# A hybrid encoder block on one core: the program that orders its instructions is given another load rate, several passes and one more place

## The chip, the cores and the metric

One core of one Trainium2 chip runs the whole block in one launch. The metric is the device time of a run in microseconds (us), as a median over several runs. All arithmetic is in 32-bit floats; products on TensorE are made exact enough by splitting each factor into a high and a low part and multiplying three times.

## The reference, cut to what matters

x is 1024 positions by 1024 channels; there are 256 memory positions and one layer.

```python
h = rms_norm(x, pre_mix_g);  z = h @ w_in + b_in              # 1024 -> 1792 columns
y_a = pool_mixer(z[:, :256], pool_w, pool_scale)              # trailing means of 2, 4, 8, 16
y_b = spatial_gating_mixer(z[:, 256:1024], sg_ln_g, sg_ln_b, sg_w, sg_b)
y_c = conformer_conv_mixer(z[:, 1024:], conv_w, conv_b, conv_ln_g, conv_ln_b)  # 31 taps
x = x + rms_norm(concat(y_a, y_b, y_c) @ w_out, post_mix_g)
h = rms_norm(x, pre_x_g);  m = rms_norm(mem, mem_g)
x = x + rms_norm(memory_cross_attention(h, m, wq, wk, wv, wo), post_x_g)       # 4 heads
h = rms_norm(x, pre_ff_g)
x = x + rms_norm(square(relu(h @ w_ff1)) @ w_ff2, post_ff_g)                   # 4096 wide
```

## The kernel before, in words

The kernel is written as a straight list of operations, and that list isn't executed in the order in which it is written. A class `Schedule` records each operation (`record`) with its engine, an estimated cost (`_cost`), the operations it depends on, and the tiles that it touches. When all are recorded, `emit` calls `order`, which goes through a simulated clock and works out one order for all engines; the program is then emitted in that order. So each engine has a fixed queue of instructions, and on the chip it runs them in that order, waiting wherever an operand isn't there yet. Every instruction therefore carries the same line number in the profile, L161 (the call in `record`), and instructions are told apart by the names of their tiles.

The order is found greedily. For each engine, among the operations whose dependencies are all placed, `pick` takes the one with the earliest possible start; among those with the same start the one with the earliest due time. That start takes in the engine's own free time, the operands' ends plus a latency by pair of engines (`LAT`; 2100 ns behind a DMA), a lock between VectorE and GpSimd for operations that use the port they share (`op.port`), and a place for every tile that is not yet live. Due times come from a pass over the operations in the order in which they are written: TensorE's operations are due one after the other by their summed costs, all others as late as what follows them allows, going backwards along the dependencies. TensorE itself takes ties in the order of writing.

A DMA is modelled as the "sync" engine: one transfer at a time, with the cost bytes / 360 (in ns; 360 GB/s, at least 450 ns), so 1456 ns for 512 KB. On the chip, SyncE's queue only issues the transfers, and many are under way at once. A load can also not be issued before the matmul that stands 150 matmuls back in the written order (`LEAD`) has ended.

Most tiles of 4 KB per partition live in a common stock of places (`slots`, `slot`; `NS` = 49). A tile takes a place at its first operation and gives it back after its last one. Statistics of a few columns have places of their own (`small`, 24 of each width), and a few constants stand by themselves, among them `pw`, the weights of the pooling mixer split in two (2 KB per partition).

The stages, with the names that the rows use:

- Input: blocks `x` are loaded, normalised, transposed (`p0t`) and scaled into `h`. Products with `zc0` to `zc2` give the convolution's input (`zg`, `za`).
- Mixers, about 33 to 270 us: `zb` is the product with rows `zr0` to `zr7` of w_in; ScalarE copies its first part into `zt`, which TensorE transposes (`zat`) into `zaT` for the pooling mixer (`zw`, `zp`, `ph`, `pya`); VectorE forms `zz` and `yb`, transposed in `ybt`; VectorE also adds the 31 taps of the convolution in `cacc`. In the same stretch the memory tokens are transposed (`memt`, `mT`) and multiplied with wk and wv (`wkp`, `wvp`).
- The rows of wk, wv and w_out arrive as `wk0r`, `wv0r`, `out0r` and so on: SyncE loads 512 KB, ScalarE makes the high part (`wk0h`), GpSimd the low part (`wk0l`, two instructions).
- Output projection: `omp`, then per block a residual and norm (`omx`, `omt`) and transposes `om0t` to `om7t`.
- Attention: `pq` (query product, done with seven half-size products in place of eight), `sc`, softmax (`mx`, `pt`), transposed weights `pT`, `o`, and the output product `ox` with weights `wob`, `wow`, `wot`.
- Dense layer: first part `fx`, `fy`, `fz` (seven half-size products; left factors `h3a10h` to `h3a71l`, right factors `w1o` from loads `w1a` to `w1d`), whose results (`c`, `sa`, `sb`) are written to DRAM as `scr_hid`; second part `g` with loads `w2a` to `w2d` and `ha` (read back from `scr_hid`), accumulated in `acc`, and the last residual in `fx` (`finish`).

Of the kernel before, what the change touches and what calls it, by code (L numbers as in the profile page):

```python
# [11 lines left out]
F32R = mybir.dt.float32r  # L12
# [4 lines left out]
P = 128  # L17
# [9 lines left out]
WINDOWS = (2, 4, 8, 16)  # L27
TAPS = 31
LEAD = 150
NS = 49  # L30


class _Op:
# [32 lines left out]
class Schedule:  # L66
# [13 lines left out]
           "pool": {"act": 75, "dve": 60, "pe": 309, "pool": 102, "sync": 100},  # L80
           "sync": {"act": 2100, "dve": 2100, "pe": 2100, "pool": 2100, "sync": 2100}}
    SLACK = 50000.0
    BYDUE = ("act", "dve", "pool", "sync")
    TABLE = {AF.Sigmoid: "sigmoid", AF.Gelu_apprx_tanh: "gelu", AF.Exp: "exp"}

# [116 lines left out]
    @staticmethod  # L202
    def _cost(eng, method, args, kw, ins):
        n = 1
        for d in args[0].shape[1:]:
            n *= d
        if method == "dma_start":
            return max(450.0, n * args[0].shape[0] * 4 / 360.0)
        size = lambda a: int(np.prod(a.shape[1:]))
        if eng == "pe":  # L210
            return max(109.0, 13.4 + n * 0.4167)
        wide = [a for a in ins if size(a) > 1]
        ptrs = len(ins) - len(wide) if n > 1 else 0
        if eng == "act":
            c = 51.0 + 0.833 * n + (0.0 if ins[0].space == bass.MemoryType.PSUM else 42.0)
            return c + 93.0 * min(ptrs, 1) + (93.0 if "accum_out" in kw else 0.0)
        if eng == "pool":
            if method == "tensor_tensor":
                return 520.0 if n < 17 else 60 + 2.4 * n
            return 60 + 1.0 * n  # L220
        n = max([n] + [size(a) for a in wide])
        psum = any(a.space == bass.MemoryType.PSUM for a in ins + [args[0]])
        if not psum and len(wide) == 1 and method in ("tensor_scalar", "tensor_scalar_mul",
                                                      "tensor_copy"):
            return 69 + 0.52 * n + 61.0 * ptrs
        return 69 + 1.042 * n + 61.0 * ptrs


    def order(self):
        ops, tiles, tags = self.ops, self.tiles, self.tags  # L230
        for i, op in enumerate(ops):
            op.left, op.ready, op.end = len(op.deps), 0.0, None
            for d in op.deps:
                ops[d].users.append(i)


        due, at = [0.0] * len(ops), 0.0
        for i, op in enumerate(ops):
            if op.eng == "pe":
                at += op.cost  # L240
            due[i] = at + (0.0 if op.eng == "pe" else self.SLACK)
        for i in range(len(ops) - 1, -1, -1):
            op = ops[i]
            for u in op.users:
# [2 lines left out]
        for i, op in enumerate(ops):  # L247
            op.due = due[i] if op.eng in self.BYDUE else op.prio
        ready = {e: [] for e in self.ENG}
# [3 lines left out]
        free = {e: 0.0 for e in self.ENG}  # L253
        port = {"dve": 0.0, "pool": 0.0}
        table = None
        out = []
        best = {e: None for e in self.ENG}
# [46 lines left out]
        n = len(ops)  # L304
        while len(out) < n:
            b, be = None, None
            for e in self.ENG:
                if ready[e]:
                    k = pick(e)
# [4 lines left out]
            t0, _, i = b  # L314
            op = ops[i]
# [3 lines left out]
            for t in op.tiles:  # L319
                r = tiles[t]  # L320
                if not r["live"]:
                    r["live"] = True
                    tag = tags[r["tag"]]
                    at = min(tag["free"])
# [11 lines left out]
            for t in op.tiles:  # L336
                r = tiles[t]
# [32 lines left out]
def block_kernel(ctx: ExitStack, tc: tile.TileContext, x, mem, pre_mix_g, w_in, b_in, pool_w,  # L370
# [4 lines left out]
    sc = Schedule(nc, LEAD)  # L375
    act, dve, pool, pe, sync = sc.act, sc.dve, sc.pool, sc.pe, sc.sync

    cp = ctx.enter_context(tc.tile_pool(name="const", bufs=1))
# [5 lines left out]
    junk = cp.tile([P, D], F32, tag="junk", name="junk")  # L384
    sc.slots(sp, NS, junk)

    def slot(name, shape, dt=F32):
        return sc.slot(name, shape, dt)
# [1 line left out]
    def bank(name):  # L390
        return sc.tile(pp, [P, 512], F32, "b", 8, name)

    def small(name, n, bufs=24):
        return sc.tile(mp, [P, n], F32, f"m{n}", bufs, name)

    x, mem, out = x[0], mem[0], out[0]
# [20 lines left out]
    def rstd_of(name, src, n, extra=None):  # L417

        t = small(name + "e", n)
        if extra is None:  # L420
            dve.tensor_scalar(t, src, EPS, None, ALU.add)
        else:
            dve.scalar_tensor_tensor(t, src, EPS, extra, ALU.add, ALU.add)
        r = small(name + "r", n)
        pool.tensor_tensor(r, t, half[:, :n], ALU.pow)
        return r
# [227 lines left out]
    for g in range(4):  # L654
        o = (g % 2) * 64
        sync.dma_start(pwr[o:o + 64, g // 2, o:o + 64], pool_w[0, g])
    pw = sc.tile(cp, [P, 2, 2, P], F32R, "pw", 1, "pw")
    act.copy(pw[:, 0], pwr)
    lo_of(dve, pw[:, 1], pwr, pw[:, 0])
    inv = sc.tile(cp, [P, 2, 16], F32, "inv", 1, "inv")  # L660
# [47 lines left out]
    for hf in range(2):  # L708
# [4 lines left out]
        for pr in range(2):  # L713
# [4 lines left out]
            for i in range(2):  # L718
# [19 lines left out]
                r = rstd_of(f"vr{hf}{b}", mv[:, 1:2], 1)  # L738
# [37 lines left out]
    for t in range(2):  # L776
# [4 lines left out]
        r = rstd_of(f"memr{t}", ms, 1)  # L781
# [512 lines left out]
    for ch in range(2):  # L1294
# [17 lines left out]
        for i, g, first in ((1, 0, True), (2, 1, True), (6, 0, False), (5, 1, True), (7, 0, False),  # L1312
                            (3, 1, False), (4, 0, False)):
            ops = []
# [20 lines left out]
            n = 1 if ch == 1 and i == 4 else 3  # L1335
# [60 lines left out]
```

## Time and profile before

| what | us |
|---|---|
| median of 3 runs | 1198.07 |
| lowest and highest run | 1197.9, 1200.57 |
| the profiled execution's own time | 1196.5 |
| its span from first to last instruction | 1194.8 |

The mean granted TensorE clock over the span is 0.994. The profile is that of one execution. A busy TensorE is one with a matmul under way; an idle stretch is put down to what ended it. The idle stretches of the other engines matter only where TensorE waits for them in the end.

### The profile page before, as it was taken

What the parts mean: (1) busy time and instruction counts of PE and PEld (TensorE: products, weight loads), DVE (VectorE), ACT (ScalarE), POOL (GpSimd) and SP (SyncE); (2) the same over time, 40 slices, a digit from 0 to 9 for tenths busy, and PEclk for the clock granted to TensorE, in tenths of its full rate; (3) what the DMA queues carried; (4) which work ended last, traced back from release to release, by engine and by line L of the source; (5) the groups of instructions that cost most, each with busy time, mean ns of one, the idle gap of its engine ahead of it and who ended that gap; (6) DMA issues with size and microseconds to landing.
All of it is one profiled execution on the core that took longest, in us unless ns stands there. A gap on an engine that the chain in (4) does not pass through costs nothing.

```text
span 1194.8 us, 14793 instructions
## 1 busy us (share of the span) xinstructions
PE 1158.2 (97%) x5387; PEld 957.9 (80%) x5387; DVE 875.1 (73%) x1234; ACT 556.2 (47%) x973; POOL 271.0 (23%) x260
## 2 busy tenths in 40 slices
PE   7999999999999999999999999999999999999997
PEld 6788877787877898788778878888888888888885
DVE  5899999464459757799996877667589744587736
ACT  6422245734566358749833434333364632435421
POOL 5352458894062403443000000000000000000001
PEclk9999999999999999999999999999999999999999
DMA  8400024652240313126043355444685244443443
GB/s 275 152 1 1 1 91 164 243 207 89 88 159 28 114 53 107 58 101 229 36 159 123 141 192 169 159 149 142 211 301 210 89 141 169 167 168 132 144 156 141
DMA packets 86056, 163.11 MB, mean 137 GB/s; under 512 B 6475, under 2 KB 29919, under 8 KB 85983
## 3 DMA queue, kind: packets, MB, share of 16 engines
q1 hardware_dynamic: 85982, 162.17, 39.1%
q8 instruction: 42, 0.69, 0.2%
q14 instruction: 32, 0.25, 0.1%
HBM read 116.01 MB, written 46.14 MB: 136 GB/s over the span
## 4 chain that ended last, share of the span: by engine, by line
PE 76%; DVE 9%; ACT 6%; DMA 4%; POOL 2%; issue 2%; SPq 1%; DVEq 0%; ACTq 0%; POOLq 0%
PE g L161 25%; PE fx L161 13%; PE fz L161 7%; PE zb L161 5%; PE ox L161 4%; PE omp L161 4%; PE pq L161 4%; PE zg L161 3%; PE za L161 2%; PE fy L161 2%; DVE cacc L161 2%; PE wkp L161 2%; ACT h L161 1%; PE sc L161 1%; ACT junk L161 1%
## 5 line engine op out<-in xcount | busy, mean ns | idle before, releaser
L161 POOL TENSOR_TENSOR fr0r<-fr0e,half 128x1 f32<-128x1 f32 x1 | 0.9, 866 | 590.2 <-DVE fr0e L161 590.2
L161 DVE SCALAR_TENSOR_TENSOR cacc<-hc,taps,cacc 128x512 f32<-128x512 f32 (+14 forms) x180 | 121.0, 738 | 0.2
L161 DVE TENSOR_TENSOR c<-c,fz 128x512 f32<-128x512 f32 x32 | 21.8, 684 | 52.2 <-PE fz L161 34.1
L161 DVE TENSOR_TENSOR acc<-acc,g 128x512 f32<-128x512 f32 x40 | 25.8, 681 | 33.1 <-PE g L161 33.1
L161 ACT COPY c<-fx 128x512 f32<-128x512 f32 x48 | 28.4, 596 | 38.6 <-PE fx L161 29.2
L161 ACT ACTIVATE c<-fx 128x512 f32<-128x512 f32 x16 | 9.6, 598 | 61.0 <-PE fx L161 61.0
L161 ACT CAST w1o<-w1a 128x512 fp32r<-128x512 f32 x32 | 20.3, 638 | 29.4 <-DVE sb L161 7.8
L161 DVE SCALAR_TENSOR_TENSOR c<-c 128x512 f32<-128x512 f32 x48 | 32.5, 684 | 0.3
L161 PE MATMUL sc<-kv,q 128*128 128x256 f32 x192 | 30.3, 291 | 0.0
L161 ACT ACTIVATE junk<-acc 128x512 f32<-128x512 f32 x16 | 10.1, 632 | 40.8 <-DVE acc L161 40.6
L161 PE MATMUL fx<-h3a40h,w1o 128*128 128x512 f32 x64 | 25.4, 397 | 2.2 <-ACT c L161 2.2
L161 PEld LDWEIGHTS sc<-kv,q 128*128 128x128 f32 x192 | 26.0, 190 | 0.9
L161 ACT CAST w1o<-w1c 128x512 fp32r<-128x512 f32 x32 | 19.6, 626 | 14.2 <-PE fz L161 5.3
L161 PE MATMUL o<-pT,kv 128*128 128x512 f32 x96 | 24.9, 394 | 1.4 <-DVE pT L161 1.4
L161 PE MATMUL fx<-h3a60h,w1o 128*128 128x512 f32 x64 | 25.3, 401 | 0.0
L161 PE MATMUL fx<-h3a11h,w1o 128*128 128x512 f32 x64 | 25.2, 393 | 0.0
L161 PE MATMUL fz<-h3a30h,w1o 128*128 128x512 f32 x64 | 25.1, 392 | 0.0
L161 PE MATMUL fy<-h3a21h,w1o 128*128 128x512 f32 x64 | 25.0, 393 | 0.0
L161 PE MATMUL fy<-h3a20h,w1o 128*128 128x512 f32 x64 | 24.9, 390 | 0.0
L161 PE MATMUL fz<-h3a50h,w1o 128*128 128x512 f32 x64 | 24.9, 389 | 0.0
L161 PE MATMUL fx<-h3a41h,w1o 128*128 128x512 f32 x64 | 24.9, 389 | 0.0
L161 PE MATMUL fz<-h3a31h,w1o 128*128 128x512 f32 x64 | 24.9, 389 | 0.0
(1555 smaller groups left out, 3991.5 us busy)
## 6 DMA issues: line engine op xcount, KB each, us to landing
ha<-scr_hid SPq DMA_DIRECT2D x56, 512.0 KB
scr_hid<-c SPq DMA_DIRECT2D x48, 256.0 KB
scr_hid<-sa SPq DMA_DIRECT2D x32, 256.0 KB
scr_hid<-sb SPq DMA_DIRECT2D x32, 256.0 KB
x<-in_x_dram SPq DMA_DIRECT2D x8, 512.0 KB
omx<-in_x_dram SPq DMA_DIRECT2D x8, 512.0 KB
scr_x<-omx SPq DMA_DIRECT2D x8, 512.0 KB
wqb<-in_wq_dram SPq DMA_DIRECT2D x8, 512.0 KB
```

The costliest lines, as they stand in the source:

```text
L161: op.fn = lambda: f(*[put(a) for a in args], **{k: put(v) for k, v in kw.items()})
```

## The change

Five things change, and no operation of the computation is added, removed or altered.

- `_cost` of a DMA becomes bytes / 250 in place of bytes / 360, so 2097 ns for 512 KB; the least cost of 450 ns and the latency of 2100 ns stay. It holds for loads and for stores.
- `order` calls the old procedure (now `_order`) six times. The first pass takes TensorE's operations in the order of writing for the due times, as before. Each later pass takes the order in which the pass before it placed TensorE's operations. The pass with the shortest simulated span is emitted. Ties on TensorE itself are still broken by the order of writing.
- The stock of 4 KB places grows from 49 to 50 (`NS`).
- `small` has 20 places of each width in place of 24.
- `pw` is no longer a constant by itself; it takes one of the 4 KB places, from its first write until the pooling mixer's last product.

```diff
--- before.py
+++ after.py
@@ -27,7 +27,7 @@
 WINDOWS = (2, 4, 8, 16)
 TAPS = 31
 LEAD = 150
-NS = 49
+NS = 50
 
 
 class _Op:
@@ -80,6 +80,7 @@
            "pool": {"act": 75, "dve": 60, "pe": 309, "pool": 102, "sync": 100},
            "sync": {"act": 2100, "dve": 2100, "pe": 2100, "pool": 2100, "sync": 2100}}
     SLACK = 50000.0
+    PASSES = 6
     BYDUE = ("act", "dve", "pool", "sync")
     TABLE = {AF.Sigmoid: "sigmoid", AF.Gelu_apprx_tanh: "gelu", AF.Exp: "exp"}
 
@@ -205,7 +206,7 @@
         for d in args[0].shape[1:]:
             n *= d
         if method == "dma_start":
-            return max(450.0, n * args[0].shape[0] * 4 / 360.0)
+            return max(450.0, n * args[0].shape[0] * 4 / 250.0)
         size = lambda a: int(np.prod(a.shape[1:]))
         if eng == "pe":
             return max(109.0, 13.4 + n * 0.4167)
@@ -227,18 +228,47 @@
 
 
     def order(self):
+
+
+        best, pe = None, [i for i, op in enumerate(self.ops) if op.eng == "pe"]
+        for n in range(self.PASSES):
+            out = self._order(pe)
+            self.spans = getattr(self, "spans", []) + [self.span]
+            if best is None or self.span < best[0]:
+                best = (self.span, out, [op.end for op in self.ops],
+                        {k: r["at"] for k, r in self.tiles.items()})
+            pe = [i for i in out if self.ops[i].eng == "pe"]
+        self.span, out, ends, places = best
+        for op, end in zip(self.ops, ends):
+            op.end = end
+        for k, at in places.items():
+            self.tiles[k]["at"] = at
+        return out
+
+    def _order(self, pe_order):
         ops, tiles, tags = self.ops, self.tiles, self.tags
+        for op in ops:
+            op.users = []
         for i, op in enumerate(ops):
             op.left, op.ready, op.end = len(op.deps), 0.0, None
             for d in op.deps:
                 ops[d].users.append(i)
-
-
-        due, at = [0.0] * len(ops), 0.0
+        for tag in tags.values():
+            tag["free"] = [(0.0, i) for i in range(tag["bufs"])]
+        for r in tiles.values():
+            r.update(left=len(r["ops"]), end=0.0, live=False, at=0)
+
+
+        due, at = [None] * len(ops), 0.0
+        for i in pe_order:
+            at += ops[i].cost
+            due[i] = at
+        at = 0.0
         for i, op in enumerate(ops):
             if op.eng == "pe":
-                at += op.cost
-            due[i] = at + (0.0 if op.eng == "pe" else self.SLACK)
+                at = max(at, due[i])
+            else:
+                due[i] = at + self.SLACK
         for i in range(len(ops) - 1, -1, -1):
             op = ops[i]
             for u in op.users:
@@ -390,7 +420,7 @@
     def bank(name):
         return sc.tile(pp, [P, 512], F32, "b", 8, name)
 
-    def small(name, n, bufs=24):
+    def small(name, n, bufs=20):
         return sc.tile(mp, [P, n], F32, f"m{n}", bufs, name)
 
     x, mem, out = x[0], mem[0], out[0]
@@ -654,7 +684,7 @@
     for g in range(4):
         o = (g % 2) * 64
         sync.dma_start(pwr[o:o + 64, g // 2, o:o + 64], pool_w[0, g])
-    pw = sc.tile(cp, [P, 2, 2, P], F32R, "pw", 1, "pw")
+    pw = slot("pw", [2, 2, P], F32R)
     act.copy(pw[:, 0], pwr)
     lo_of(dve, pw[:, 1], pwr, pw[:, 0])
     inv = sc.tile(cp, [P, 2, 16], F32, "inv", 1, "inv")
```

## Rows read from the trace of the kernel before

**Rows 1.** The profile page: span, and busy us (share) xinstructions by engine.

```profile
span 1194.8 us, 14793 instructions
PE 1158.2 (97%) x5387; PEld 957.9 (80%) x5387; DVE 875.1 (73%) x1234; ACT 556.2 (47%) x973; POOL 271.0 (23%) x260
```

**Rows 2.** Waits of TensorE: waiter <- releaser: total us, times, longest us.

```profile
PE gmixp L161 <- DMA gmixr<-in_pre_mix_g_dram: 5.9, 1, 5.9
PE fx L161 <- DVE h3a70l L161: 3.2, 1, 3.2
PE ybt L161 <- DVE zz L161: 2.9, 2, 2.4
PE fx L161 <- ACT c L161: 2.4, 3, 1.5
PE zat L161 <- ACT zt L161: 2.1, 1, 2.1
PE om6t L161 <- DVE omt L161: 1.5, 1, 1.5
PE o L161 <- DVE pT L161: 1.4, 1, 1.4
...
PE pT L161 <- DVE pt L161: 1.3, 1, 1.3
...
PE memt L161 <- ACT zaT L161: 0.7, 1, 0.7
...
PE omp L161 <- POOL out6l L161: 0.3, 1, 0.3
```

**Rows 3.** Windows: length; busy us (count) by engine; clock; DMA share; GB/s.

```profile
182.00:184.00 2.00, 2.00 (x11) 1.65 (x10) 2.00 (x4) 1.06 (x1) 2.00 (x3) 1.00 0.99 338
...
190.00:192.00 2.00, 1.30 (x7) 0.96 (x6) 1.97 (x7) 2.00 (x7) 1.60 (x3) 0.59 0.01 2
...
214.00:216.00 2.00, 2.00 (x7) 1.64 (x7) 0.61 (x2) 1.96 (x3) 2.00 (x3) 0.56 1.04 424
```

**Rows 4.** Timeline of ScalarE: start, us, operation [idle before <- what ended it].

```profile
4.35 1.06 ACT L161 ACTIVATE junk<-x 128x1024 f32<-128x1024 f32 x1 [2.27 <-DMA x<-in_x_dram]
...
186.93 1.04 ACT L161 CAST wk6h<-wk6r 128x1024 fp32r<-128x1024 f32 x1 [0.24 <-DMA wk6r<-in_wk_dram]
187.88 0.37 ACT L161 COPY zt<-zb 128x256 f32<-128x256 f32 x1
...
210.54 1.04 ACT L161 CAST wv3h<-wv3r 128x1024 fp32r<-128x1024 f32 x1 [2.45 <-DMA wv3r<-in_wv_dram]
```

**Rows 5.** Timeline of SyncE's queue: when each transfer was issued.

```profile
0.80 0.86 SPq L161 DMA_DIRECT2D x<-in_x_dram  x2
...
173.66 0.33 SPq L161 DMA_DIRECT2D wk0r<-in_wk_dram  x1
...
179.83 0.33 SPq L161 DMA_DIRECT2D wk6r<-in_wk_dram  x1
...
203.49 0.33 SPq L161 DMA_DIRECT2D wv2r<-in_wv_dram  x1
204.84 0.33 SPq L161 DMA_DIRECT2D wv3r<-in_wv_dram  x1
```

**Rows 6.** Windows, sum from 175 to 271 us.

```profile
sum 96.00, PE 90.05 PEld 72.93 DVE 63.47 ACT 54.03 POOL 83.10; mean PE 12.86 PEld 10.42 DVE 9.07 ACT 7.72 POOL 11.87
```

**Rows 7.** The tile pt (min/median/max ns), then the timeline around 475 us.

```profile
L161 DVE TENSOR_SCALAR pt<-pt,rs x32: 334/349/2540, 434.1 to 481.9; 128x256 f32<-128x256 f32 x32
...
476.06 2.38 POOL L161 TENSOR_TENSOR wot<-wob,wob 128x1024 f32<-128x1024 f32 x1
```

**Rows 8.** Windows at the change from attention to the dense layer.

```profile
550.00:560.00 10.00, 10.00 (x50) 8.28 (x49) 8.98 (x13) 9.97 (x28) 0.55 (x1) 1.00 1.04 336
...
590.00:600.00 10.00, 5.93 (x24) 4.02 (x23) 10.00 (x11) 5.07 (x8) 0.00 (x0) 1.00 0.00 1
600.00:604.00 4.00, 4.00 (x12) 3.13 (x11) 4.00 (x6) 1.33 (x3) 0.00 (x0) 0.58 0.00 0
```

## The prediction

> **What bounds the kernel now.** I read the page's busy times first: TensorE is busy for 1158.2 of 1194.8 us, VectorE for 73% [rows 1]. So the kernel is bound by TensorE, and an order of instructions can win at most the 36.6 us in which TensorE stands idle, and what the idle stretches cost it in clock. No product is added or removed, so nothing else is to be had on that engine.
>
> Second, TensorE's waits [rows 2]. 5.9 us go to the first load at the very start; that is before any order can help. Of those that could move, the largest are `fx <- h3a70l` 3.2, `ybt <- zz` 2.9, `fx <- c` 2.4, `zat <- zt` 2.1, `om6t <- omt` 1.5, `o <- pT` 1.4, `pT <- pt` 1.3 and `memt <- zaT` 0.7: 15.5 us together. In none of them is a DMA named. The releaser is always another engine that came late, and the question is what that one had waited for.
>
> Third, the windows just behind the largest of these idle stretches, for the granted clock. After the `zat` and `memt` waits it is 0.59 over 190 to 192 us, after the `ybt` waits 0.56 over 214 to 216 us [rows 3], after `h3a70l` 0.58 over 600 to 604 us [rows 8]: TensorE at its lower level, 1.2 GHz. Over those last 4 us the share lost is 0.42, so 1.7 us of work. I take 1.7 us for each of the three, an estimate from the one stretch that is seen whole. With it the three idle stretches are worth 2.1 + 0.7 + 1.7 = 4.5 us, 2.9 + 1.7 = 4.6 us, and 3.2 + 1.7 = 4.9 us.
>
> Fourth, the timelines of ScalarE and SyncE's queue, for what made the releasers late. TensorE waited for `zat` until ScalarE had copied `zt` (187.88). Ahead of `zt` in ScalarE's queue stood `wk6h`, which waited for the load of `wk6r`, issued at 179.83, until 186.93 [rows 4, 5]: 7.1 us after the issue. It stood there because the program that made the order believed that this load would be there sooner. At 210.54 ScalarE waits in the same way for `wv3r`, for 2.45 us [rows 4].
>
> **The change part by part.**
>
> *Loads at 250.* A load of 512 KB is now booked at 2.10 us in place of 1.46, with 2.1 us of latency behind it in both. Six of them stand in a row from `wk0r` at 173.66 [rows 5] to `wk6r` (`wk1r` had gone before). By the old booking the last lands at 173.66 + 6 x 1.46 + 2.1 = 184.5; by the new one at 188.3; on the chip it was 186.9. For `wv3r`, the second from 203.49 [rows 5], the old booking gives 208.5, the new one 209.8, the chip 210.5. So where loads come in crowds the old figure was early by about 2 us and the new one is off by 1.4 us late and 0.7 us early. In the first case the sign turns, and that matters: the greedy order gives ScalarE the instruction that can start first, and with the load at 188.3 that is `zt`. The head of the queue no longer blocks. Worth: 4.5 us in full, nothing at the least.
>
> For the stall at 210 the new figure is still a little early, and VectorE's `zz` is late for another reason too (it stands behind `zp`, which runs while GpSimd holds the shared port). Worth: 4.6 us at most, half of it by the chip's own load times.
>
> What is late next if both go? GpSimd. From 175 to 271 us it is busy for 83.1 of 96 us [rows 6], with the low parts of all rows of wk, wv and w_out, and at 270 us TensorE already waits 0.3 us for `out6l` [rows 2]. All of TensorE's work behind the mixers feeds on these low parts, and their number is fixed. So TensorE can come out of this stretch earlier only by as much as GpSimd's 12.9 us of idle time shrink, and part of that is before the first row has landed. I take half of it, 6.5 us, as the cap, and 4.0 us of the 9.1 as the value, since the second stall goes only in part. Ends: 0 and 9.1.
>
> *The same figure elsewhere.* `fx <- c` (2.4 us in three waits) stands behind ScalarE's high parts of loads in the dense layer, and `om6t <- omt` (1.5) behind GpSimd's low part of a load of wq. Sum 3.9 us; they are single waits of the same kind, but the late load isn't always the one ahead, so I take half, 2.0. Ends 0 and 3.9.
>
> *Ties by TensorE's own order.* The due time decides only among instructions of an engine that could start at the same moment, so it counts where an engine is full and has a choice. That is VectorE around 590: busy for 10.00 of 10 us while TensorE does 5.93 [rows 8]. There the choice can bring `h3a70l` ahead of low parts that are needed later, but VectorE's sum of work doesn't shrink. I take 1.0 us of the 4.9, ends 0 and 4.9. Should the first pass turn out the shortest, the passes do nothing, and this 1.0 is lost.
>
> *One more place, `pw` in a place, 20 small ones.* Up to the pooling mixer's end the fiftieth place is taken by `pw`, so there the stock is what it was; only behind 216 us is there one more. In the dense layer's second part TensorE doesn't stall as it is, so it has nothing to win there. The small tiles live for a few instructions of one norm each. I take nothing for all three, covered by SyncE's queue being ahead of its users; if that cover is gone, a load that waits for a place is late by one low part, 1.3 us, either way.
>
> *What the new order breaks.* This isn't an edit at one place: every queue is dealt anew. Waits that come of a slip between plan and chip will come again elsewhere. The tile `pt` shows how: normalising takes 0.35 us, but 2.54 once, while GpSimd's `wot` holds the port [rows 7], and TensorE waits 1.3 us. The three of this family, `om6t`, `o` and `pT`, make 4.2 us now. The new order removes old ones and brings new ones: ends +4.2 (as many again on top) and -2.7 (the last two gone, nothing new). I take a loss of 1.7, nearer to the middle.
>
> *The sum.* 4.0 + 2.0 + 1.0 - 1.7 = 5.3 us. The profiled execution's own time was 1196.5, so 1191.2 by it. That execution is 1.57 us below the median of 1198.07; set against the median the forecast is 1192.8.
>
> **The rivals.**
>
> *A. GpSimd takes it back (same).* The 4.0 us are won at 190 and 212 and lost again by 271, since GpSimd works on without a break. For it: 83.1 of 96 us busy and the 0.3 us wait at its end [rows 2, 6]. Against it: GpSimd itself waits for high parts that stand behind late loads. Time: 1198.07 - (5.3 - 4.0) = 1196.8.
>
> *B. 250 is the wrong figure (same).* The first two loads of x are issued at 0.80, and ScalarE has the first at 4.35 [rows 4, 5], 3.55 us later. The old booking gives 1.46 + 2.1 = 3.56, the new one 4.20. In dense stretches the queues move 338 GB/s at a share of 0.99 [rows 3] and 336 at 1.04 [rows 8]. So for a load by itself and for the sum of many 360 was right; only a single load within a crowd is late. A plan that is too slow puts consumers later in the queues than they need to be, and at the start all waits for loads. It costs about 0.64 us for each load that gates something; with the six further blocks of x, 3.8 us, which come off the gain: 1198.07 - 5.3 + 3.8 = 1196.6. The Trainium skill, in "DMA: Bandwidth & Descriptors", section Specifications, gives about 358 GB/s as the limit of HBM for one core and 368 as a cost model's figure; by that rule 360 should have stayed, and the rates just named agree with it, while the 7.1 us of `wk6r` don't.
>
> *C. The change into the dense layer gets worse (slower).* Between 550 and 560 us the DMA engines are full (share 1.04) and VectorE is at 8.98 of 10; from 580 it has no slack at all [rows 8]. The eight loads of w1 and, ahead of them in the same queue, the four stores of the first half's blocks to `scr_x` are each booked 0.64 us longer; in the plan the last load ends 7.7 us later, and VectorE's low parts and sums of w1 can be put behind the `h3` work. Each us of VectorE's work that moves out of 550 to 570 into 580 to 600 is a us more of TensorE's wait, and a new idle stretch of some us brings the low clock again. Price: 7.7 + 1.7 = 9.4 us, in place of the gain of 1.0 there: 1198.07 - 4.3 + 9.4 = 1203.2. It decides against the change from 4.3 us on, that is, once some 2.6 us of VectorE's work have moved; 550 to 560 has 1.02 us without work for it now. Against it: on the chip the loads land no later than before, and a queue in order loses nothing where its next instruction is ready.
>
> *D. All goes well.* Terms near their good ends under GpSimd's cap: 6.5 + 3.9 + 2.5 = 12.9 us, 1185.2.
>
> **How the numbers follow.** About 0.3% (3.6 us) is what a measurement can tell from no change here, so faster ends at 1194.5 and slower begins at 1201.7. The forecast, 1192.8 with its own range from 1189 to 1196, has 0.47; A 0.18; B 0.10; C 0.18; D 0.07. Faster: 0.40 of the forecast, D, and 0.04 of the others make 0.51. Slower: most of C (0.13) and the part of the forecast's, A's and B's cases in which the collisions are at their bad end, 0.06, make 0.19. The rest, 0.30, is within. The range takes in D's end and C's figure: 1185 to 1204. I choose the forecast for the row of `wk6h`: the largest late releaser is explained by the booked load to within 2 us.
>
> **What would show it.** Right: `zt` ahead of `wk6h` in ScalarE's queue, no `zat` wait, no low clock at 190; TensorE's idle sum near 31 us; `omp` at 270 earlier by about 4 us. GpSimd without idle time between 190 and 270 and `omp` where it was is A. ScalarE's or VectorE's waits at the start longer is B. More than 7 us of TensorE idle between 550 and 610 is C. Wrong altogether would be new waits on DMAs in the dense layer's second part, where TensorE has none now, or another order of products on TensorE that changes what is short in each stretch.

## The result and the profile after

The changed kernel takes 1183.93 us (median; 1182.68 to 1184.12) beside 1197.99 us for the kernel before in the same batch: a ratio of 0.9882, 95% interval 0.9856 to 0.9908. It is 14.1 us faster. The forecast was 5.3 us, and 1183.93 lies below the lower end of the range, 1185.

The page of after, span and busy us by engine:

```profile
span 1182.3 us, 14750 instructions
...
PE 1154.1 (98%) x5387; PEld 957.0 (81%) x5387; DVE 882.1 (75%) x1234; ACT 554.7 (47%) x973; POOL 262.2 (22%) x260
```

Set against [rows 1], the span is 12.5 us shorter. TensorE's idle time accounts for 8.4 of these (36.6 to 28.2 us) and its busy time for 4.1 (1158.2 to 1154.1). The products are the same 5387, so most of the second part is clock. Apart from one over the last 4 to 5 us, which both have, before had three stretches at the lower level and after has one; at 1.7 us each, the prediction's estimate, the two that are gone make 3.4 of the 4.1 us.

TensorE's waits of after (waiter <- releaser: total us, times, longest us):

```profile
PE pT L162 <- DVE pt L162: 4.4, 3, 2.1
...
PE om6t L162 <- DVE omt L162: 1.2, 1, 1.2
...
PE fx L162 <- DVE h3a70l L162: 0.4, 1, 0.4
...
PE omp L162 <- POOL out6l L162: 0.3, 1, 0.3
```

Of the waits in [rows 2], `zat`, `ybt` and `fx <- c` are gone and `h3a70l` has shrunk from 3.2 to 0.4. One has grown: `pT <- pt`, from 1.3 to 4.4.

Windows of after (length; busy us and count of TensorE, its loads, VectorE, ScalarE, GpSimd; clock; DMA share; GB/s), at the places of [rows 3, 6, 8] and in attention:

```profile
175.00:265.00 90.00, 88.11 (x432) 71.00 (x431) 61.47 (x118) 53.39 (x80) 84.13 (x72) 1.00 0.62 216
190.00:192.00 2.00, 2.00 (x9) 1.68 (x10) 1.99 (x4) 2.00 (x4) 2.00 (x4) 1.00 0.00 0
466.00:470.00 4.00, 2.01 (x13) 1.45 (x11) 4.00 (x3) 1.92 (x5) 3.92 (x3) 1.00 0.00 0
470.00:474.00 4.00, 2.64 (x9) 2.20 (x10) 3.96 (x9) 2.12 (x6) 1.06 (x1) 0.61 0.00 0
590.00:600.00 10.00, 9.60 (x41) 7.29 (x40) 10.00 (x12) 4.62 (x8) 0.00 (x0) 1.00 0.33 102
600.00:604.00 4.00, 4.00 (x19) 3.31 (x18) 4.00 (x6) 1.60 (x4) 0.00 (x0) 1.00 0.04 13
```

TensorE no longer falls to its lower clock at 190 and 600 us. It falls at 470 instead, behind a stretch in which GpSimd and VectorE are full and TensorE does 2.01 of 4 us.

**Where the time went.** Every version deals the queues anew, so waits can't be matched one to one. I put the traces on a common scale: each matmul counts as its columns / 2.4 ns plus 11 ns (at least 60 ns), and I read when each kernel has done the same amount of that work. The table gives the change of a kernel's lag against before within each stretch, in us, with the stretches by before's time. Negative is a gain. It is worked out from the matmul starts of one profile per kernel; the last column is the lag at 913 us, after which the spans differ by no more than a few tenths from it. Executions of one kernel differ too, and the profiled one can lie off the median (that of passes_place took 1197.84 us, its median is 1195.72), so a cell of less than some 2 us shows little by itself.

| kernel | to 183 (start) | 183-279 (mixers) | 279-407 | 407-515 (attention) | 515-626 (into the dense layer) | 626-913 | sum |
|---|---|---|---|---|---|---|---|
| after | -0.2 | -6.4 | -1.2 | +4.1 | -5.8 | -3.4 | -12.8 |
| rate_only | 0.0 | -4.8 | +0.4 | +6.1 | +1.0 | -3.0 | -0.4 |
| passes_only | -0.3 | -4.6 | +1.1 | -1.3 | -5.4 | +1.4 | -9.1 |
| place_only | 0.0 | -1.4 | +0.2 | -1.4 | -1.1 | -2.2 | -5.8 |
| rate_place | 0.0 | -4.9 | -0.2 | +2.6 | +3.7 | -3.3 | -2.2 |
| rate_passes | -0.2 | -6.4 | -0.2 | +7.5 | -5.4 | -3.0 | -7.6 |
| passes_place | +0.2 | -0.7 | +2.5 | +2.3 | +0.2 | -2.7 | +1.8 |
| rows_at_250 | -0.1 | -2.2 | +0.7 | 0.0 | +1.0 | +0.3 | -0.3 |
| wo_at_250 | +0.4 | +1.6 | 0.0 | +2.4 | +3.9 | +0.4 | +8.8 |
| zt_first | -0.3 | -0.6 | -0.5 | 0.0 | -0.1 | +2.6 | +1.0 |
| casts_behind | -0.1 | -0.3 | -0.5 | 0.0 | 0.0 | +0.5 | -0.3 |
| wo_at_360 | -0.2 | -6.4 | -1.2 | +5.3 | +1.3 | -3.4 | -4.6 |
| quiet_wo | -0.4 | -6.4 | -0.8 | -2.8 | -5.8 | -3.4 | -19.5 |
| wo4_on_vector | -0.2 | -6.4 | -0.8 | -1.3 | -5.8 | -3.4 | -17.7 |
| pt_on_scalar | -0.3 | -6.4 | -1.3 | +6.6 | -5.8 | -3.3 | -10.5 |
| after_pass3 | -0.3 | -3.5 | +1.8 | +4.3 | -4.2 | -3.2 | -5.0 |
| rate_225 | +8.1 | -3.2 | -1.1 | -0.2 | -6.3 | -2.9 | -5.6 |
| rate_275 | -0.5 | -0.3 | +0.8 | +5.8 | -5.1 | -2.5 | -1.8 |
| rate_300 | +6.3 | -4.5 | +1.1 | -1.0 | -4.0 | -2.0 | -4.0 |

### The profile page after: what moved, and what is told of

The parts are those of the page before. It is cut to its first block, busy times and chain, and to the rows that moved or that the text cites. A ratio compares the mean times of both kernels' runs of the same rounds, so it can differ in the third digit from the quotient of the medians.

```text
span 1182.3 us, 14750 instructions
## 1 busy us (share of the span) xinstructions
PE 1154.1 (98%) x5387; PEld 957.0 (81%) x5387; DVE 882.1 (75%) x1234; ACT 554.7 (47%) x973; POOL 262.2 (22%) x260
## 4 chain that ended last, share of the span: by engine, by line
PE 85%; DVE 8%; ACT 3%; issue 1%; POOL 1%; DMA 0%; DVEq 0%; ACTq 0%; POOLq 0%
PE g L162 26%; PE fx L162 13%; PE fz L162 7%; PE omp L162 6%; PE pq L162 6%; PE zb L162 5%; PE ox L162 4%; PE zg L162 3%; PE za L162 3%; PE fy L162 3%; PE wkp L162 2%; DVE cacc L162 2%; PE wvp L162 2%; PE o L162 1%; PE sc L162 1%; ACT h L162 1%
## 5 line engine op out<-in xcount | busy, mean ns | idle before, releaser
L162 DVE SCALAR_TENSOR_TENSOR cacc<-hc,taps,cacc 128x512 f32<-128x512 f32 (+19 forms) x180 | 122.0, 764 | 0.1
L162 PE MATMUL fx<-h3a10h,w1o 128*128 128x512 f32 x64 | 24.9, 390 | 0.0
L162 PE MATMUL fz<-h3a51h,w1o 128*128 128x512 f32 x64 | 24.8, 389 | 0.0
```

Of the source, the lines that this page charges most:

```text
L162: op.fn = lambda: f(*[put(a) for a in args], **{k: put(v) for k, v in kw.items()})
```

## The experiments

Ratios are to the kernel before within the same batch, with 95% intervals.

### The parts of the change, alone and in pairs

**The rate alone**, on the kernel before:

```diff
-            return max(450.0, n * args[0].shape[0] * 4 / 360.0)
+            return max(450.0, n * args[0].shape[0] * 4 / 250.0)
```

> The kernel before with transfers booked at 250 in place of 360 GB/s, and nothing else. Theory 1 (late loads): the booking removes the waits in the mixers (zat, ybt and the low clock behind them) and in the dense layer, so most of the 14 us is here: 1188 to 1190, without the zat wait, but with the 3.2 us wait for h3a70l at the entry to the dense layer. Theory 2 (passes): the load rate matters little, the time stays within 3 us of 1198. Theory 3 (a new deal): any change of the booking gives another order whose time lies anywhere within 6 us of 1196, with waits that have no pattern.

1195.86 us, 0.9987 (0.9977 to 0.9996).

**The six passes alone**: after with `/ 360.0`, `NS = 49`, 24 small tiles, `pw` in its own place.

> The kernel before with six passes, at 360 GB/s, 49 places, pw by itself. Theory 1 (late loads): the zat and ybt waits behind late loads stay, since the booking is the old one, and only the tie-breaking at the entry to the dense layer gains: 1192 to 1194, the 3.2 us wait for h3a70l gone. Theory 2 (passes): 1186 or less. Theory 3 (a new deal): within 6 us of 1196.

1188.77 us, 0.9930 (0.9916 to 0.9945).

**The place alone**: before with `NS = 50`, 20 small tiles and `pw` in a place.

> The kernel before with 50 places, 20 small tiles and pw in a place; 360 GB/s, one pass. Theories 1 and 2: no stall goes for it, 1196 to 1199. Theory 3 (a new deal): the order changes all the same, so within 6 us of 1196, and the stalls sit elsewhere.

1190.34 us, 0.9942 (0.9925 to 0.9958).

**Rate and place**, which is after with one pass:

```diff
-    PASSES = 6
+    PASSES = 1
```

> The changed kernel with one pass in place of six (250 GB/s, 50 places, pw in a place, 20 small tiles). Theory 1 (late loads): nearly all of the gain stays, 1186 to 1189. Theory 2 (passes): the gain goes, 1194 to 1198. Theory 3 (a new deal): within 6 us of 1192.

1193.79 us, 0.9971 (0.9961 to 0.9981).

**Rate and passes**: after with `NS = 49`, 24 small tiles, `pw` in its own place.

> 250 GB/s and six passes, but 49 places, pw by itself and 24 small tiles. If the three parts add up: 1196.5 - 1.5 - 8.6 = 1187 to 1188. If the loss in attention goes with 250 and the gain at the entry to the dense layer with the passes: mixers 5 to 7 us shorter, attention 4 to 6 longer, the entry 6 shorter, 1187 to 1191. Theory 3 (a new deal): anywhere from 1183 to 1195.

1189.12 us, 0.9934 (0.9917 to 0.9950).

**Passes and place**: after with 360 in place of 250.

> The changed kernel with 360 in place of 250. If the parts add up: 1197.4 - 8.6 - 7.0 = 1181 to 1183, so faster than the changed kernel. If place and passes win the same waits (the entry to the dense layer): 1187 to 1189. Theory 1 in its second form: the zat wait is back (1.7 to 2.1 us), no low clock in attention.

1195.72 us, 0.9989 (0.9979 to 0.9998).

The waits that tell these kernels apart, one fence for each (TensorE's waits of rate_only, then passes_only, place_only, rate_place and passes_place):

```profile
PE pT L161 <- DVE pt L161: 6.0, 4, 2.0
...
PE fx L161 <- DVE h3a70l L161: 3.2, 1, 3.2
```

```profile
PE zat L162 <- ACT zt L162: 1.8, 1, 1.8
```

```profile
PE ybt L161 <- DVE zz L161: 3.2, 2, 2.7
PE zat L161 <- ACT zt L161: 1.7, 1, 1.7
```

```profile
PE fx L162 <- DVE w1o L162: 4.3, 1, 4.3
PE pT L162 <- DVE pt L162: 3.6, 3, 1.9
```

```profile
PE pT L162 <- DVE rs L162: 3.7, 1, 3.7
...
PE fx L162 <- DVE h3a70l L162: 1.8, 1, 1.8
PE zat L162 <- ACT zt L162: 1.7, 1, 1.7
```

Two things follow. First, the parts don't add up. By the medians of each batch, rate alone gives 1.5 us, passes 8.6, place 7.0, which would be 17; the three pairs give 3.6, 8.1 and 1.5; all three give 14.1. Place on top of the rate and passes is worth some 6 us, place on top of the passes is a loss of about 7. No part has a value of its own: each deals the whole order anew.

Second, by stretch there is a pattern nevertheless. The wait of `zat` for `zt` stays at 1.7 to 1.8 us where the rows of wk are booked at 360 (passes, place, and both) and isn't among the long ones where they are booked at 250. The rate alone gives 4.8 us in the mixers, close to the 4.0 forecast for it, and then loses 6.1 us in attention to the wait for `pt`.

### Is 250 a better figure, or another draw?

**225, 275 and 300 GB/s**, with the passes and the place as in after; only the divisor changes.

> The changed kernel with 225 in place of 250 GB/s. If the time follows the booked rate up to the point where it meets the chip's own crowds of loads (6.9 to 7.1 us for one of 512 KB): 1182 to 1186, no zat wait. If each rate is another deal: anywhere from 1180 to 1197.

> The changed kernel with 275 in place of 250 GB/s. If the time follows the booked rate: 1186 to 1188, no zat wait. If each rate is another deal: anywhere from 1180 to 1197.

> The changed kernel with 300 in place of 250 GB/s. If the time follows the booked rate (360: 1195.7, 250: 1183.9): about 1190, with a short zat wait. If each rate is another deal: anywhere from 1180 to 1197.

| rate | 225 | 250 (after) | 275 | 300 | 360 (passes_place) |
|---|---|---|---|---|---|
| us | 1190.93 | 1183.93 | 1194.51 | 1194.17 | 1195.72 |
| ratio | 0.9939 | 0.9882 | 0.9982 | 0.9975 | 0.9989 |
| 95% | 0.9921-0.9957 | 0.9856-0.9908 | 0.9970-0.9993 | 0.9962-0.9988 | 0.9979-0.9998 |

250 stands alone. A figure 10% to either side costs 7 and 10.6 us, while the other four lie within 5 us of each other. If 250 fitted the chip's own rate, I would expect the gain to fall off gently to either side, and in the same stretches. It doesn't: 225 and 300 lose 8.1 and 6.3 us by 183 us, where 250 and 275 lose nothing, and 275 then gains only 0.3 us in the mixers. The loss of the two is an earlier `ybt`, near 157 us, that waits twice for `zz`: 3.0 and 1.9 us at 225, 3.0 and 1.6 us at 300, each with 6.8 us at the lower clock, from 158.1 and 155.1 us. At 275, TensorE waits 3.9 us in the mixers for `mT` and is at the lower clock for 10.2 us from 188.6.

**After with three passes**, `PASSES = 3`.

> The changed kernel with three passes, so that the third pass is emitted in place of the fifth; its simulated span is 2.7 us longer by the procedure's own account. If the choice of the shortest pass carries over to the chip: 1186 to 1188. If a pass is only another deal: anywhere from 1180 to 1196, with the zat wait gone in any case.

1190.15 us, 0.9942 (0.9925 to 0.9959). The order that after uses comes from its fifth pass. The best of three is another, which the ordering procedure itself reckons 2.7 us longer (1170.0 against 1167.2, as each kernel's `order` gives it); on the chip it is 6.2 us longer. The procedure's own spans rank the kernels only loosely. The three orders that it reckons shortest (passes_only 1166.9, after 1167.2, rate_passes 1167.7) are the three fastest of the fourteen that it made, but the next, passes_place at 1168.1, is among the slow ones; and it gives 1175.1 for 225 and 1173.3 for 275, of which the chip runs the first 3.6 us faster.

### Which loads carry the effect

**Only the loads of wk, wv and w_out at 250**, on before, in the recording of an operation:

```diff
         op.cost = self._cost(...)
+        if method == "dma_start" and isinstance(args[0], _Slot):
+            if args[0].name.startswith(("s:wk", "s:wv", "s:out")):
+                op.cost = max(450.0, int(np.prod(form(args[0]).shape)) * 4 / 250.0)
```

> The kernel before with only the loads of the rows of wk, wv and w_out booked at 250; all other transfers stay at 360. Theory 1 in its second form (the booking gains about 5 us in the mixers and loses about 5 in attention): the zat wait is gone, the mixers are 4 to 5 us shorter, attention as before: 1191 to 1194. Theory 3 (a new deal): the gain in the mixers comes, but the stages behind it change too by up to 5 us either way.

1196.83 us, 0.9997 (0.9987 to 1.0006). TensorE's waits:

```profile
PE ybt L161 <- DVE zz L161: 4.1, 2, 3.6
```

`zat` isn't among its waits, as the booked load predicts, and `ybt` takes it over: 4.1 us in place of 2.9. Of the gain of 2.2 us in the mixers, some 0.5 are left at 626 us.

**Only attention's loads of wo at 250**, on before: the same edit with `("s:wob",)`.

> The kernel before with only the eight loads of wo booked at 250. Theory 1 in its second form: everything up to the scores as before, then the waits of the transposes pT for pt grow from 1.3 to 4 to 6 us and a stretch at the low clock comes with them: 1201 to 1204. Theory 3 (a new deal): attention changes by less than 2 us, since the loss of the kernels at 250 came of what the order was before that stage.

1203.84 us, 1.0055 (1.0040 to 1.0070), the only kernel that is clearly slower. TensorE's waits:

```profile
PE fx L161 <- DVE w1o L161: 5.5, 1, 5.5
PE pT L161 <- DVE pt L161: 3.7, 3, 1.9
```

**Only attention's loads of wo back at 360**, on after: the same edit with `("s:wob",)` and 360.

> The changed kernel with the eight loads of wo booked at 360 again. If the 250 for wo alone makes the loss in attention: the pT waits are under 1.5 us, no low clock at 470, 1179 to 1181, faster than both kernels. If any change deals anew and the stage before that stays: mixers as in the changed kernel, then 1180 to 1192.

1190.79 us, 0.9943 (0.9923 to 0.9963). Up to 407 us it runs as after does. Attention doesn't improve (+5.3 against +4.1), and the gain at the dense layer's entry is gone (+1.3 against -5.8). So this one booking can bring the wait for `pt`, but taking it back doesn't take the wait away.

### What the two stalls of the mixers are worth by themselves

**`wk6h` behind `zt`**: before's own order, with ScalarE's `wk6h` moved to right behind the copy of `zt`.

```diff
-        order = self.order()
+        order = list(self.order())
+        # src: ScalarE's wk6h; dst: the next ScalarE instruction on zt11
+        order[src:dst + 1] = order[src + 1:dst + 1] + [order[src]]
```

> The kernel before, its order as it was on every engine, but for one instruction: ScalarE's wk6h goes right behind zt instead of ahead of it. If the late load at the head of ScalarE's queue makes the zat wait: the 2.1 us wait and the low clock at 190 go, TensorE is 4 to 4.5 us earlier there, and 1 to 4 us of it are left at the end (1193 to 1196), since GpSimd or the wait at 212 takes back some. If that wait has another cause (zb itself, VectorE): no change at 190, 1196 to 1199.

1197.10 us, 1.0004 (0.9991 to 1.0018). `zt` now starts at 186.62 in place of 187.88 and the wait of `zat` is 1.1 us in place of 2.1, but the low clock stays, now from 191.2 us: neither of the two cases. 1.6 us of gain reach 626 us. Behind it 2.6 are lost, with a new stretch at the lower clock at 706.6 us.

**`wk5h` and `wk6h` behind `zt`** and the seven ScalarE instructions after it, by the same kind of move.

> The kernel before, its order kept on every engine but ScalarE: the two casts wk5h and wk6h go behind the copy zt and the seven instructions that follow it. If the late load ahead of zt is the whole of the mixers' stall at 190: the zat wait and the low clock at 190 go and TensorE is 4 to 4.5 us earlier by 200, of which 1 to 4 are left at the end, 1193 to 1196. If the stall is shared by more engines, as the move of one cast suggests (it gave 0.9 us by 200): 1 to 2 us, 1195 to 1197, with waits for mT (VectorE) in its place.

1198.03 us, 1.0005 (0.9991 to 1.0019): no change, and above both of the ranges that were given. ScalarE's timeline (start, us, operation [idle before <- what ended it]), with `zt` where after has it:

```profile
185.37 0.37 ACT L161 COPY zt<-zb 128x256 f32<-128x256 f32 x1 [0.23 <-PE zb L161]
...
188.92 1.07 ACT L161 CAST wk5h<-wk5r 128x1024 fp32r<-128x1024 f32 x1
189.86 1.09 ACT L161 CAST wk6h<-wk6r 128x1024 fp32r<-128x1024 f32 x1
```

The `zat` wait and the low clock at 190 are gone, and at 192 us TensorE is 2.2 us ahead. Then come TensorE's and GpSimd's timelines:

```profile
211.74 0.41 PE L161 MATMUL ybt<-ident,zz 128*128 128x128 f32 x2 [2.74 <-DVE zz L161]
```

```profile
197.64 4.11 POOL L161 TENSOR_TENSOR zz<-zz,sgn 128x384 f32<-128x384 f32 x4 [3.99 <-DVE zz L161]
...
208.31 1.71 POOL L161 TENSOR_TENSOR wk5l<-wk5r,wk5h 128x512 fp32r<-128x512 f32 x1
211.35 1.27 POOL L161 TENSOR_TENSOR ph<-zp,ph 128x512 fp32r<-128x512 f32 x1 [1.33 <-ACT ph L161]
212.58 1.29 POOL L161 TENSOR_TENSOR wk5l<-wk5r,wk5h 128x512 fp32r<-128x512 f32 x1
```

`ybt` starts at 211.74; in before it started at 212.00, after 2.39 us of wait. Its operand `zz` comes no sooner for TensorE's being ahead (GpSimd's part of it starts at 197.64, in before at 197.87), and TensorE has nothing to fill in, because GpSimd makes `wk5l` only after `zz` and a `ph`. So a stall taken away at 190 comes back at 210. After's GpSimd does it the other way round:

```profile
190.70 2.56 POOL L162 TENSOR_TENSOR wk5l<-wk5r,wk5h 128x512 fp32r<-128x512 f32 x2
...
194.23 2.55 POOL L162 TENSOR_TENSOR wk6l<-wk6r,wk6h 128x512 fp32r<-128x512 f32 x2
196.72 2.57 POOL L162 TENSOR_TENSOR wk7l<-wk7r,wk7h 128x512 fp32r<-128x512 f32 x2
...
202.89 4.11 POOL L162 TENSOR_TENSOR zz<-zz,sgn 128x384 f32<-128x384 f32 x4 [0.57 <-DVE zz L162]
```

With the low parts of rows 5 to 7 made by 199.3 us, TensorE runs `wkp` without a break up to its `ybt` at 212.30. `zz` is no earlier than in before, but TensorE has worked in the meantime: at 237 us it is 8.0 us ahead.

### What attention loses

After's VectorE and GpSimd around 466 us, then the tile `pt` (min/median/max ns, first and last start):

```profile
465.34 6.13 DVE L162 TENSOR_SCALAR pt<-pt,rs 128x256 f32<-128x256 f32 x4
```

```profile
463.87 2.40 POOL L162 TENSOR_TENSOR wow20l<-wob,wow20h 128x1024 fp32r<-128x1024 f32 x1 [6.41 <-ACT wow20h L162]
466.23 2.41 POOL L162 TENSOR_TENSOR wob<-wob,wob 128x1024 f32<-128x1024 f32 x1
468.72 2.34 POOL L162 TENSOR_TENSOR wot<-wob,wob 128x1024 f32<-128x1024 f32 x1
```

```profile
L162 DVE TENSOR_SCALAR pt<-pt,rs x32: 339/349/2494, 426.2 to 473.7; 128x256 f32<-128x256 f32 x32
```

Four normalisations that need 0.35 us each take 6.13 us, while three of GpSimd's instructions follow one another without a gap. Before has the same three instructions of GpSimd in a row, from 471.21 us, and two of its normalisations fall beside them, of 1.43 and 2.54 us (the second is that of [rows 7]). After has three there, of 1.08, 2.46 and 2.49 us, and one of 2.40 us at 455.2.

**GpSimd kept off**: after, with its eleven two-operand instructions on wo as memsets in the same places of the order, which leaves out part of the output product. A memset takes 0.96 us.

```diff
+        if eng == "pool" and isinstance(args[0], _Slot) and args[0].name[:5] in ("s:wow", "s:wob", "s:wot"):
+            op.fn = lambda: self.nc.gpsimd.memset(put(args[0].bitcast(F32)), 0.0)
```

> The changed kernel with its order unchanged on every engine; GpSimd's eleven two-operand instructions on wo (low parts, differences) are replaced by a memset of the same tile, so the output product is left out in part (its low parts and some factors are zero). If the shared port makes the pT waits (4.4 us, low clock at 470): they go, and the kernel ends 4 to 6 us earlier, 1178 to 1180. If they come of VectorE's own queue or of ScalarE: less than 1.5 us.

1177.40 us, 0.9837 (0.9821 to 0.9853). Windows at the two places:

```profile
466.00:470.00 4.00, 4.00 (x24) 3.46 (x24) 2.99 (x7) 3.42 (x9) 0.00 (x0) 1.00 0.00 0
470.00:474.00 4.00, 4.00 (x21) 3.26 (x21) 2.61 (x4) 4.00 (x7) 1.86 (x2) 1.00 0.01 2
```

TensorE is full in both, at full clock. Attention goes from +4.1 to -2.8 us: the two-operand instructions on GpSimd cost after 6.9 us there.

**Four of them on VectorE**, all work kept:

```diff
+        if eng == "pool" and any(n in args[0].name for n in ("wow10l", "wow20l", "wob000", "wot20")
+                                 if isinstance(args[0], _Slot)):
+            f = getattr(self.nc.vector, method)
```

> The changed kernel, its order kept; four of GpSimd's two-operand instructions on wo, the four that fall into attention (wow10l, wow20l and the differences that form wob and wot), are issued on VectorE instead, at the same place in the order. If the shared port makes the pT waits: VectorE gets 4 x 1.2 us of work but no longer waits some 6 us for the port, the pT waits fall under 2 us, 1179 to 1182, faster than both kernels. If VectorE's own work is what pt waits for: 1184 to 1188.

1179.00 us, 0.9848 (0.9830 to 0.9866), the fastest kernel here with all of the work in it. The page, then the tile `pt`:

```profile
span 1177.4 us, 14744 instructions
...
PE 1152.5 (98%) x5387; PEld 956.7 (81%) x5387; DVE 879.6 (75%) x1238; ACT 554.5 (47%) x973; POOL 253.0 (21%) x256
```

```profile
L165 DVE TENSOR_SCALAR pt<-pt,rs x32: 334/348/355, 426.7 to 470.2; 128x256 f32<-128x256 f32 x32
```

No `pt` takes more than 355 ns, and VectorE's busy time falls, from 882.1 to 879.6 us, though it has four instructions more. By stretch it equals after everywhere but in attention (-1.3 against +4.1). The intervals of the two ratios, each to before in its own batch, overlap by a tenth of a per cent; the two profiled spans differ by 4.9 us.

**The normalisation on ScalarE**, after's order otherwise:

```diff
+        if method == "tensor_scalar_mul" and isinstance(args[0], _Slot) and args[0].name[:4] == "s:pt":
+            op.fn = lambda: self.nc.scalar.activation(put(args[0]), put(args[1]), AF.Copy, scale=put(args[2]))
```

> The changed kernel, its order kept; the 32 normalisations of pt are issued on ScalarE (activation with a scale) in place of VectorE. If the shared port makes the pT waits: ScalarE doesn't use it, the waits for pt fall, but ScalarE gets 32 x 0.37 to 0.48 us more, 12 to 15 us where it has 15 to 20 us idle: 1179 to 1184. If ScalarE becomes the bound there: 1185 to 1190.

1186.41 us, 0.9911 (0.9893 to 0.9929). TensorE's waits:

```profile
PE pT L162 <- ACT pt L164: 3.2, 9, 0.8
```

The long waits and the low clock are gone, but there are nine short ones, and attention loses 6.6 us: ScalarE, which also has the exponentials, has become the one that TensorE follows. 2.5 us slower than after.

## Why the prediction was off

**What bounds it, and the sum.** That the change can win only TensorE's idle time and its clock held: 8.4 and 4.1 us make up the span's 12.5. The idle sum was forecast near 31 us and is 28.2. By stretch, forecast against measured: mixers 4.0 against 6.4; the same figure elsewhere 2.0 against 4.6 (1.2 from 279 to 407 us, 3.4 from 626 on); entry to the dense layer 1.0 against 5.8; collisions -1.7 against -4.1. Every gain was put too low, and the loss too. The sum failed by its largest miss, the third term.

**The entry to the dense layer: the step that failed.** I argued that the choice among ties can bring `h3a70l` forward but that VectorE's work there doesn't shrink, and took 1.0 of 4.9. VectorE is indeed as full as before, 10.00 of 10 us, and yet TensorE does 9.60 of them in place of the 5.93 of [rows 8]. The step from a full VectorE to a wait that mostly stays was wrong: it didn't ask what else TensorE could do until `h3a70l` is there. VectorE's timelines, in before, then after, then passes_only:

```profile
584.17 0.68 DVE L161 TENSOR_TENSOR w1o<-w1t,w1o 128x512 fp32r<-128x512 f32 x1
...
597.94 1.21 DVE L161 TENSOR_TENSOR h3a70l<-h,h3a70h 128x1024 fp32r<-128x1024 f32 x1
599.07 0.68 DVE L161 TENSOR_TENSOR w1o<-w1t,w1o 128x512 fp32r<-128x512 f32 x1
```

```profile
579.61 1.29 DVE L162 TENSOR_TENSOR w1o<-w1t,w1o 128x512 fp32r<-128x512 f32 x2
...
589.42 1.23 DVE L162 TENSOR_TENSOR h3a70l<-h,h3a70h 128x1024 fp32r<-128x1024 f32 x1
...
591.16 1.22 DVE L162 TENSOR_TENSOR h3a50l<-h3s,h3a50h 128x1024 fp32r<-128x1024 f32 x1
```

```profile
585.63 0.68 DVE L162 TENSOR_TENSOR w1o<-w1t,w1o 128x512 fp32r<-128x512 f32 x1
...
590.85 1.22 DVE L162 TENSOR_TENSOR h3a70l<-h,h3a70h 128x1024 fp32r<-128x1024 f32 x1
```

The second `w1o<-w1t` is the low part that the second of two products with `h3a6` (12 matmuls each) needs. In before it comes behind `h3a70l`: TensorE has run 14 matmuls with `h3a6` when it stops for `h3a70l`, and the other ten follow later. In after, passes_only and rate_passes it comes first, and TensorE has run all 24. In after `h3a70l` itself also stands ahead of `h3a50l` and `h3a51l`, which it stood behind, and is 8.5 us earlier, of which 3.7 are the lead that after has at 515 us anyway. But in passes_only and rate_passes it still stands behind both, so that move isn't what the gain needs. An engine that is full still chooses what its consumer gets first.

The runs tie this to the passes. In the first pass the procedure holds the second `w1o<-w1t` due at 566.1 us, behind `h3a70l` at 556.7; in the pass that after uses, at 555.0, ahead of 558.0. On before's scale it starts at 584.2 to 591.3 us in all nine orders with several passes and at 596.8 to 599.0 in the five with one. Seven of the nine gain 4.0 to 6.3 us at the entry, and none of the five more than 1.1. It isn't a law: passes_place, which still waits 1.8 us for `h3a70l`, has +0.2, and wo_at_360, which gains 3.9 us from 590 to 605, has lost it again by 626. Moving the one instruction by itself wasn't tried, so that it is the decisive one is argued and not shown. I also put the place at nothing. By itself it gave 7.0 us, of which 1.1 here, and on top of rate and passes some 6; it deals the order anew like the other parts.

**The mixers: the marks right, the prices wrong.** The marks given for it came true: `zt` at 185.32 stands ahead of `wk6h` at 190.18 in ScalarE's queue, there is no `zat` wait and no low clock at 190:

```profile
185.32 0.37 ACT L162 COPY zt<-zb 128x256 f32<-128x256 f32 x1 [0.42 <-PE zb L162]
...
190.18 1.08 ACT L162 CAST wk6h<-wk6r 128x1024 fp32r<-128x1024 f32 x1
```

But I priced the stalls at 190 and 210 as 4.5 and 4.6 us side by side. casts_behind takes the first away whole and ends where it began: the 2.2 us won at 192 are gone by 212. The other way round, passes_only keeps the first (a `zat` wait of 1.8 us and the lower clock from 188.8), has no `ybt` wait among its long ones, and gains 4.6 us in the mixers, nearly all of it between 205 and 217 us. So taking away the late load that the prediction explained was worth nothing by itself there, and the second stall, of which it hoped for half, was worth its price. In after and in passes_only GpSimd makes `wk5l` ahead of `zz`, and TensorE has work in the meantime; the prediction looked at GpSimd's order only as a cap. That order wasn't moved by itself, and rate_only loses both waits with `wk5l` behind `zz`, so it isn't the only way. As a cap it held well: I allowed 6.5 us, half of GpSimd's 12.9 idle us; its idle time fell to 5.9 (90.00 less 84.13), and of 8.0 us won by 237 us 6.6 remain at 279. So GpSimd takes back 1.4, and at the end TensorE waits 0.3 us for `out6l` as before.

**The same figure elsewhere.** 4.6 us lie 0.7 beyond my end of 3.9. The waits for `c` went, as forecast, but `om6t` is still 1.2. Eleven of the fourteen orders dealt anew gain 2.0 to 3.4 us behind 626, whatever their rate (place_only 2.2, passes_place 2.7, by the table; 225 to 300 from 2.0 to 2.9), so this loss belongs to before's order more than to the figure.

**The collisions.** 4.1 against the bad end of 4.2. The place was the one named, the tile `pt` beside GpSimd, and quiet_wo and wo4_on_vector show the cause: 6.9 us with GpSimd off it, 5.4 of them with four instructions moved. I took 1.7 because I balanced new waits against old ones. Yet attention loses 2.4 to 7.5 us in all six kernels that book wo at 250 (after_pass3 4.3 among them), while passes and place by themselves gain 1.3 and 1.4 there; wo_at_250 shows that this booking alone is enough. It isn't needed, though: passes_place loses 2.3 and wo_at_360 5.3. And a slower booking isn't worse: 225 has -0.2 there, 275 +5.8.

**The rivals.** A was right in kind and small, 1.4 us. B's evidence stands (a load by itself takes what 360 says), its price doesn't: the start is 0.2 us earlier, and in no run with all loads at 250 was it later. The Trainium skill's figure in "DMA: Bandwidth & Descriptors", section Specifications, some 358 GB/s, agrees with the 338 GB/s in the first line of [rows 3]; the 424 of the third line lie above it. C didn't happen in after. rate_place pays 3.7 us at the entry, for `w1o`, as C has it; but wo_at_250 pays 3.9 there for `w1o` too, with its loads of w1 booked at 360, so the longer booking of these loads isn't needed for it. D's 1185.2 is nearest to the result, by other terms: it had 2.5 for the entry and no loss in attention. What I gave too little weight is the spread. The fourteen orders dealt anew here run from 1183.9 to 1203.8 us, and twelve of them are faster than before by their intervals (rows_at_250 can't be told from it, wo_at_250 is slower). So its order was a poor draw among these, and a new one is a draw from about that range.

**Open.** Whether 250 holds anything beyond a lucky draw of the whole order; 225 and 275 speak against it, but three neighbours are few. Whether the second `w1o<-w1t` by itself is decisive at the entry. Why `zz` is late near 157 us at 225 and 300.

## What to carry over

When a change deals a whole order anew, don't add up the stalls that it may remove: follow each to the next wait on the same engine, and ask whether that one ends at a fixed moment. If it does, the gain stops there unless the engine gets other work to fill in. Where the releaser is full, ask which one of its instructions would give the waiting engine something else to do. And before tuning the figures of an ordering procedure, look for a pair of engines that hold each other up in one stretch: moving four instructions gave 4.9 us, and seven of the fourteen orders dealt anew gave less than that against before.

## What was not expected of the hardware

- VectorE's `tensor_scalar` of 128x256 takes 0.35 us, and up to 2.49 us beside GpSimd's two-operand instructions of 2.4 us, mostly about as long as one of these. In [rows 7] I took it for a single event, but before already has a second one, of 1.43 us, beside it; where more of the normalisations meet GpSimd's three in a row it is repeated, four in 6.13 us.
- The low clock doesn't answer to a stretch's idle time alone in these traces. In casts_behind TensorE does 0.94 of the 2 us from 190 to 192 with the granted clock at 1.00; before does 1.30 there at 0.59, behind a wait of 2.1 us:

```profile
190.00:192.00 2.00, 0.94 (x5) 0.46 (x4) 0.65 (x2) 2.00 (x5) 2.00 (x3) 1.00 0.00 0
```

The same kernel has 0.50 from 214 to 216 us, behind its wait of 2.74 us. The stretches at the lower level last 3.4 us in most of the traces, 6.8 in some (rate_only at 473.1 and 599.4 us) and 10.2 in rate_275 at 188.6; my 1.7 us for each was right for those of 3.4.
